# Front of an encoder layer: a fifth gate unit's first products among the last transposes, weight sums behind token sums, tables made 25 products later

## The chip, the cores and the metric

The kernel runs on one core of a Trainium2 chip. The metric is the device time of one execution in microseconds, as the median of several runs. One execution was also taken by the hardware profiler, and every view below is of that one.

## What is computed

One encoder layer on 1024 tokens of 1024 features, in 32-bit floats. Only the first line matters for this change; the rest is cut.

```python
u = rms_norm(h, norm_mix)
proj = u @ w_in                       # 1024 x 3328
z_pool, q, k, v, g_pool, g_attn = split(proj)
y_pool = multiscale_pool(z_pool, w_pool_group, pool_scale) @ w_pool_branch
y_attn = windowed_gqa(q, k, v, sink) @ w_attn_branch
h = h + (sigmoid(g_pool) * y_pool + sigmoid(g_attn) * y_attn) @ w_out
...
```

## The kernel before

**The input projection** is cut into 13 units of 256 output columns: eight gate units ("g", 0) to ("g", 7), z01 and z23 (pooled branch), kv, q01 and q23. Each unit is a 2 x 2 block product (token halves by feature halves) done with seven products instead of eight, in the order `ORDER = ("P1", "P2", "P5", "P6", "P7", "P3", "P4")`. P1 and P2 take the transposed first token half as it is (A11, A12). The other five take sums of the halves: S1, S2, S3, S4 and A22. Some of the weight blocks must be subtracted from each other too; `less` in `block_weights` (L142) does that on GpSimd.

**Each 32-bit operand is split** into a high part (a cast on ScalarE, L84) and a low part (what is left, a subtraction on VectorE, L85, or on GpSimd for the first four weight chunks). One product is 4 blocks of 128 features by 3 matmuls (high by high, high by low, low by high), so 12 matmuls of 512 columns in TensorE (L181). The list `sequence` gives the order of all products; `ahead(n)` loads and splits the weights of the next n of them.

**The front** is the loop over eight rows of 128 tokens, t = 0 to 7. For each row: load x, square and sum it on ScalarE (L417), one over the root on GpSimd (L233), scale by it and by the gain on VectorE (the tile ut, L421), then transpose in TensorE (L379) into one PSUM bank per 512 features, and split that bank. Rows 0 to 3 give A11 and A12. Rows 4 to 7 meet the rows 0 to 3 that were kept (f1, f2 are the halves of the kept row, u1, u2 those of the new one):

```python
        to("S1", combine(s, u1, u2, ALU.add))
        to("A22", u2)
        d = combine(u1, f1, u1, ALU.subtract)
        to("S3", d)
        s2 = combine(f1, s, f1, ALU.subtract)
        to("S2", s2)
        to("S4", combine(f2, f2, s2, ALU.subtract, nc.vector))
```

The first three sums (the token sums s, d and s2) are on GpSimd, the last on VectorE (L392 for all four). Between the transposes stand products that need A11 and A12 alone: P1 and P2 of units 0 to 3. A gate unit's P2 ends in a sigmoid on ScalarE (L301) into the one buffer c11, and a store from there to DRAM. After the loop come P5 of unit 0 and all others; from there on TensorE has operands for everything.

**Small tables** are made after the loop: the distance table for the attention bias (an iota on GpSimd, L449, and four VectorE operations, L450 to L453), the negated sink logits (L459), the pooled branch's weights (L461 to L465) and the counts at its edges (L466 to L474).

**What sets the order.** The framework traces the program, and a scheduler writes one queue per engine when the kernel is built. Each engine runs its queue in that order, and waits at the first instruction whose operands or buffers are not there. `tc.issue_after(ins)` puts what is traced under it behind `ins`, for instructions on the engine of `ins` alone. Tiles of one tag share `bufs` buffers: ut has six, so rows 6 and 7 take buffers that earlier rows have left; the eight PSUM banks are shared by products and transposes.

## Time and profile before

| | |
|---|---|
| time, median of 3 runs | 1187.93 us (1187.76 to 1191.13) |
| time of the profiled execution | 1189.52 us |
| its span, first to last instruction | 1187.7 us |
| TensorE busy | 1155.4 us, 97% |
| VectorE, ScalarE, GpSimd busy | 852.8, 531.2, 484.4 us |

The time of the profiled execution is its span and 1.8 us around it; it lies 1.6 us above the median. Engines are named as in the profile: PE is TensorE, DVE VectorE, ACT ScalarE, POOL GpSimd, SP the engine that issues most loads. L numbers are lines of the kernel before. An operation's row says when it began and how long it took, and in brackets how long the engine had been idle and what ended that.

### The profile page before, as it was taken

Reading aid. Unit: us, or ns where it says so; the run is one execution under the profiler, and the core shown is the slowest. Engines: PE = TensorE matmul, PEld = TensorE weight load, DVE = VectorE, ACT = ScalarE, POOL = GpSimd, SP = SyncE. Lnnn points to the kernel's source line nnn. Section 1 sums busy time; section 2 is a strip of 40 time slices with the busy share of each in tenths; the row PEclk is TensorE's granted clock in tenths of the full one; section 3 lists DMA queues with packets and bytes.
Section 4 is the critical chain, followed back from the end, with each engine's and each line's share of the span. In section 5 each row is a group of like instructions: output and inputs, shape, how many; then the busy total and the mean of one; then the engine's idle time right before and its main releaser. Section 6 shows DMA issues by size and latency. Waiting matters only on the chain.

```text
span 1187.7 us, 15579 instructions
## 1 busy us (share of the span) xinstructions
PE 1155.4 (97%) x5284; PEld 957.7 (81%) x5284; DVE 852.8 (72%) x1297; ACT 531.2 (45%) x1017; POOL 484.4 (41%) x451
## 2 busy tenths in 40 slices
PE   7899999999999999999999999999999999999995
PEld 6788888888888878888778888888888878888884
DVE  6944697765999795549878776777777774665773
ACT  6534345545677544536323333332333344454453
POOL 6833344453545551204444644555544620020230
PEclk9999999999999999999999999999999999999998
DMA  6334235138531665624355543544445357655472
GB/s 213 102 121 137 77 124 180 51 109 303 178 116 45 193 202 190 228 87 152 98 194 191 174 158 128 194 159 160 150 160 179 132 208 268 243 196 193 159 253 84
DMA packets 135347, 192.65 MB, mean 162 GB/s; under 512 B 8866, under 2 KB 87714, under 8 KB 135268
## 3 DMA queue, kind: packets, MB, share of 16 engines
q1 hardware_dynamic: 124276, 157.85, 40.8%
q0 software_dynamic: 7440, 24.39, 5.5%
q10 hardware_dynamic: 3552, 9.44, 2.2%
q8 instruction: 41, 0.67, 0.2%
q14 instruction: 38, 0.31, 0.1%
HBM read 136.85 MB, written 54.79 MB: 161 GB/s over the span
## 4 chain that ended last, share of the span: by engine, by line
PE 83%; DVE 9%; DMA 3%; issue 3%; ACT 1%; POOL 1%; SPq 0%; POOLq 0%; DVEq 0%; ACTq 0%
PE dn L828 17%; PE Z L181 14%; PE X L181 13%; PE Y L181 13%; PE wo L981 7%; PE W L181 7%; DVE wlo L85 2%; PE br L213 2%; PE br L214 2%; PE br L212 2%; DMA sums<-in_w_ffn_down_dram 2%; PE pt L669 1%; PE sc L646 1%; PE pv L682 1%; PE sc L645 1%
## 5 line engine op out<-in xcount | busy, mean ns | idle before, releaser
L84 ACT CAST whi<-raw 128x512 fp32r<-128x512 f32 x378 | 231.2, 619 | 347.0 <-POOL raw L142 79.5
L85 DVE TENSOR_TENSOR wlo<-raw,whi 128x512 fp32r<-128x512 f32 x358 | 323.4, 911 | 63.3 <-ACT whi L84 58.1
L142 POOL TENSOR_TENSOR raw<-raw 128x512 f32<-128x512 f32 x140 | 192.5, 1377 | 229.9 <-DVE wlo L85 191.5
L828 PE MATMUL dn<-wlo,ah 128*128 128x512 f32 x308 | 119.8, 389 | 0.3 <-DVE wlo L85 0.3
L828 PE MATMUL dn<-whi,ah 128*128 128x512 f32 x308 | 117.7, 389 | 1.0 <-ACT ah L84 1.0
L828 PE MATMUL dn<-whi,al 128*128 128x512 f32 x308 | 118.2, 389 | 0.0
L85 DVE TENSOR_TENSOR al<-ab,ah 128x512 fp32r<-128x512 f32 x69 | 48.6, 704 | 67.8 <-ACT ah L84 67.7
L84 ACT CAST ah<-ab 128x512 fp32r<-128x512 f32 x69 | 42.9, 622 | 87.9 <-PE dn L828 87.7
L181 PE MATMUL X<-S_hi,wlo 128*128 128x512 f32 x192 | 75.6, 393 | 0.2 <-DVE wlo L85 0.2
L1053 DVE TENSOR_TENSOR sums<-sums 128x256 f32<-128x256 f32 x88 | 51.0, 580 | 34.0 <-DMA sums<-in_w_ffn_down_dram 30.2
L181 PE MATMUL X<-S_lo,whi 128*128 128x512 f32 x192 | 75.4, 393 | 0.0
L181 PE MATMUL X<-S_hi,whi 128*128 128x512 f32 x192 | 75.3, 392 | 0.0
L181 PE MATMUL Z<-a,whi 128*128 128x512 f32 (+1 forms) x240 | 70.4, 378 | 0.1
L181 PE MATMUL Z<-A_hi,whi 128*128 128x512 f32 x176 | 68.7, 390 | 0.0
L181 PE MATMUL Z<-A_lo,whi 128*128 128x512 f32 x176 | 68.7, 390 | 0.0
L828 PEld LDWEIGHTS dn<-whi,ah 128*128 128x128 f32 x308 | 57.8, 188 | 13.3 <-ACT ah L84 1.4
L181 PE MATMUL Z<-A_hi,wlo 128*128 128x512 f32 x176 | 68.5, 389 | 0.0
L828 PEld LDWEIGHTS dn<-wlo,ah 128*128 128x128 f32 x308 | 57.8, 188 | 12.8 <-DVE wlo L85 0.8
L828 PEld LDWEIGHTS dn<-whi,al 128*128 128x128 f32 x308 | 57.8, 188 | 12.0
L181 PE MATMUL W<-S,whi 128*128 128x512 f32 x176 | 54.6, 391 | 1.8 <-ACT S L84 1.8
L1206 POOL TENSOR_TENSOR o<-o,gain_fin 128x512 f32<-128x512 f32 x8 | 12.4, 1569 | 106.1 <-ACT junk L903 106.1
L659 POOL TENSOR_SCALAR s<-s,den 128x384 f32<-128x384 f32 (+1 forms) x32 | 39.0, 1229 | 38.9 <-DVE den L657 29.3
(265 smaller groups left out, 2802.0 us busy)
## 6 DMA issues: line engine op xcount, KB each, us to landing
ab<-act_dram SPq DMA_DIRECT2D x31, 512.0 KB, 4.0
raw<-in_w_in_dram SPq DMA_DIRECT2D x26, 512.0 KB, 3.8
raw<-in_w_ffn_gate_dram SPq DMA_DIRECT2D x22, 512.0 KB, 4.3
raw<-in_w_ffn_up_dram SPq DMA_DIRECT2D x22, 512.0 KB, 3.9
sums<-in_w_ffn_down_dram SPq DMA_DIRECT2D x44, 256.0 KB, 4.6
wt_dram<-sums SPq DMA_DIRECT2D x22, 512.0 KB, 2.8
act_dram<-sums POOLq DMA_DIRECT2D x44, 256.0 KB, 2.8
raw<-wt_dram SPq DMA_DIRECT2D x20, 512.0 KB, 4.4
```

What stands on the lines that cost most here:

```text
L84: ins = nc.scalar.copy(out=hi, in_=src)
L85: (eng or nc.vector).tensor_tensor(out=lo, in0=src, in1=as32(hi), op=ALU.subtract)
L142: nc.gpsimd.tensor_tensor(out=out, in0=x0, in1=x1, op=ALU.subtract)
L181: nc.tensor.matmul(ps, wt[:, c], at[:, k, cols], start=opening and k == 0 and i == 0, stop=k == 3 and i == 2, skip_group_check=not opening)
L212: nc.tensor.matmul(ps, wh, xh, start=first, stop=False)
L213: nc.tensor.matmul(ps, wh, xl, start=False, stop=False)
L214: nc.tensor.matmul(ps, wl, xh, start=False, stop=last)
L659: (nc.gpsimd if i in POOL_HEADS else nc.vector).tensor_scalar(out=s[:, i, :W], in0=s[:, i, :W], scalar1=den[:, i:i + 1], scalar2=None, op0 ...
L828: nc.tensor.matmul(ps[t], at[:, ts], wt, start=opening and k == 0 and e == 0, stop=k == nk - 1 and e == 2, skip_group_check=not opening)
L981: nc.tensor.matmul(ps[t], at[:, k, ts], wt, start=k == 0 and e == 0, stop=k == KT - 1 and e == 2)
L1053: nc.vector.tensor_tensor(out=out, in0=in0, in1=in1, op=op)
L1206: nc.gpsimd.tensor_tensor(out=o[t][:, :HALF], in0=o[t][:, :HALF], in1=gain3[:, :HALF], op=ALU.mult)
```

## The change

**Products.** Gate unit 4 becomes a fifth early unit: its P1 is traced in row 7 between the transposes for S3 and S2, its P2 right after the loop. Its five other products come after those of units 0 and 1; those of units 2 and 3 move behind z23. The products of row t, for t from 4, are traced ahead of the row's transposes and no longer behind them. The count of products is the same. The tile s1 of the fifth unit gets a pool of its own, and goes before the pooled branch's tiles are made.

**GpSimd.** The weight subtractions of early units are put behind the token sum that was traced last.

**Tables.** Their code moves into `open_pooled`, called before P1 of z01; on VectorE they stand behind the addition of unit 4's P6.

**Squares.** The square's unused result is written to the row's ut tile, not to a tile of its own, and the copies of the gain stand behind both halves of row 0.

```diff
         def less(out, x0, x1):
-            nc.gpsimd.tensor_tensor(out=out, in0=x0, in1=x1, op=ALU.subtract)
+            with ExitStack() as stack:
+                if unit in early_units and "sum" in state:
+                    stack.enter_context(tc.issue_after(state["sum"]))
+                nc.gpsimd.tensor_tensor(out=out, in0=x0, in1=x1, op=ALU.subtract)
             return out
...
         elif prod == "P6":
-            nc.vector.tensor_tensor(out=sb[unit, "s1"], in0=ps, in1=sb[unit, "s1"], **add)
+            state["add"] = nc.vector.tensor_tensor(out=sb[unit, "s1"], in0=ps, in1=sb[unit, "s1"], **add).ins
...
-    early_units = [("g", i) for i in range(4)]
+    early_units = [("g", i) for i in range(5)]
...
     sequence = [(u, p) for i in range(2) for p in ORDER[:2] for u in early_units[2 * i:2 * i + 2]]
+    sequence += [(early_units[4], p) for p in ORDER[:2]]
     sequence += [(u, p) for p in ORDER[2:] for u in early_units[:2]]
-    sequence += [(u, p) for u in early_units[2:] for p in ORDER[2:]]
-    for u in ("z01", "z23", ("g", 4), ("g", 5), "kv", "q01"):
-        sequence += [(u, p) for p in ORDER]
+    for u in (early_units[4], "z01", "z23", early_units[2], early_units[3], ("g", 5), "kv", "q01"):
+        sequence += [(u, p) for p in ORDER[2 if u in early_units else 0:]]
...
     def in_tile(tag, unit):
+        if (tag, unit) == ("s1", early_units[4]):
+            return fifth.tile([P, HALF], F32, name="s1")
...
+    fifth = tc.alloc_tile_pool(name="fifth", bufs=1)
     xin = tc.alloc_tile_pool(name="xin", bufs=1)
...
         def combine(out, in0, in1, op, eng=nc.gpsimd):
-            eng.tensor_tensor(out=out, in0=in0, in1=in1, op=op)
+            ins = eng.tensor_tensor(out=out, in0=in0, in1=in1, op=op).ins
+            if eng is nc.gpsimd:
+                state["sum"] = ins
             return out
...
         to("S3", d)
+        if t == 7:
+            in_product(*sequence[8])
+            ahead(1)
         s2 = combine(f1, s, f1, ALU.subtract)
...
-        junk = xin.tile([P, D], F32, tag="junk", bufs=1, name="junk")
+        ut = xin.tile([P, D], F32, tag="ut", bufs=6, name="ut")
         ssq = small.tile([P, 1], F32, tag="ssq", bufs=2, name="ssq")
...
-            nc.scalar.activation(out=junk, in_=xt, func=AF.Square, accum_out=ssq)
+            nc.scalar.activation(out=ut, in_=xt, func=AF.Square, accum_out=ssq)
         rstd = rstd_of(ssq)
-        ut = xin.tile([P, D], F32, tag="ut", bufs=6, name="ut")
...
         if t == 0:
-            for half in range(2):
-                nc.vector.tensor_copy(out=gain[:, half_of(half)], in_=gains[half])
+            with tc.issue_after(normed):
+                for half in range(2):
+                    nc.vector.tensor_copy(out=gain[:, half_of(half)], in_=gains[half])
+        if t >= 4:
+            in_product(*sequence[t])
+            ahead(1)
         block_columns(t, ut)
...
-        if t >= 4:
-            in_product(*sequence[t])
-            ahead(1)
+    in_product(*sequence[9])
+    ahead(1)
     xin.release()
...
+    def open_pooled():
...
+        both = const.tile([P, D], F32, tag="gain", bufs=1, name="dist")
+        dist, far = pooled["dist"] = both[:, :3 * P], both[:, 3 * P:6 * P]
+        dist_i = far.bitcast(I32)
+        with tc.issue_after(state["add"]):
+            nc.vector.tensor_scalar(out=nsink, in0=sink_b, scalar1=-1.0, scalar2=None, op0=ALU.mult)
+            split(wg_raw, *wg)
+            nc.vector.tensor_copy(out=edge_n, in_=edge_i)
+            nc.vector.reciprocal(out=edge_n, in_=edge_n)
+            nc.gpsimd.iota(dist_i, pattern=[[-1, 3 * P]], base=P, channel_multiplier=1)
+            nc.vector.tensor_copy(out=dist, in_=dist_i)
+            nc.vector.tensor_scalar(out=far, in0=dist, scalar1=-1.0, scalar2=None, op0=ALU.mult)
+            nc.vector.tensor_tensor(out=dist, in0=dist, in1=far, op=ALU.max)
+            nc.vector.tensor_scalar(out=far, in0=dist, scalar1=float(P), scalar2=-NEG, op0=ALU.is_gt, op1=ALU.mult)
...
-        if i < NT:
+        if i < NT + 2:
             continue
+        if (unit, prod) == ("z01", "P1"):
+            fifth.release()
+            open_pooled()
```


**In the order, first: VectorE and ScalarE, rows 5 to 7.** Rows 4, 5, 6 and 7 are the tiles ut_407, ut_479, ut_552 and ut_625 before. On VectorE the S4 sum of row 5 is written in ut_204, the kept row 1:

```order
L421 SCALAR_TENSOR_TENSOR ut_552<-xt_324,rstd_550,gain_mix_89 128x1024
L85 TENSOR_TENSOR A22_lo_118<-tp_418,A22_hi_117 128x4x128
L85 TENSOR_TENSOR S3_lo_114<-tp_426,S3_hi_113 128x4x128
L85 TENSOR_TENSOR S2_lo_112<-tp_434,S2_hi_111 128x4x128
L421 SCALAR_TENSOR_TENSOR ut_625<-xt_449,rstd_623,gain_mix_89 128x1024
L85 TENSOR_TENSOR wlo_397<-raw_394,whi_396 128x512
L392 TENSOR_TENSOR ut_204<-ut_204 128x512
L85 TENSOR_TENSOR S4_lo_116<-tp_442,S4_hi_115 128x4x128
```

With the change rows 4 to 7 are ut_399, ut_470, ut_539 and ut_608, and the kept row 1 is ut_199:

```order
L85 TENSOR_TENSOR wlo_390<-raw_387,whi_389 128x512
L85 TENSOR_TENSOR S1_lo_110<-tp_430,S1_hi_109 128x4x128
L398 TENSOR_TENSOR ut_199<-ut_199 128x512
L85 TENSOR_TENSOR A22_lo_118<-tp_437,A22_hi_117 128x4x128
L85 TENSOR_TENSOR S3_lo_114<-tp_445,S3_hi_113 128x4x128
L234 TENSOR_SCALAR ms_542<-ssq_540 128x1
L85 TENSOR_TENSOR wlo_396<-raw_393,whi_395 128x512
L431 SCALAR_TENSOR_TENSOR ut_539<-xt_323,rstd_544,gain_mix_89 128x1024
```

The S4 sum of row 5 stood behind the scaling of rows 6 and 7 and a weight split; now it stands ahead of the scaling of row 6, and that of row 7 comes nine instructions later still. On ScalarE the squares of rows 6 and 7 stood ahead of the first transposes of row 4:

```order
L84 CAST a1_107<-tp_317 128x4x128
L417 ACTIVATE junk_545,ssq_546<-xt_324 128x1024
L417 ACTIVATE junk_618,ssq_619<-xt_449 128x1024
L84 CAST S1_hi_109<-tp_411 128x4x128
L84 CAST whi_384<-raw_382 128x512
```

With the change row 6's square is behind the high parts of row 4, and row 7's stands here, behind the sigmoids of units 0 and 1 (c11_363 and c11_378 share one buffer):

```order
L306 ACTIVATE c11_363<-Z_223 128x512
L84 CAST whi_424<-raw_422 128x512
L306 ACTIVATE c11_378<-Z_238 128x512
L84 CAST whi_495<-raw_493 128x512
L190 COPY s1_420<-Z_407 128x512
L84 CAST S2_hi_111<-tp_453 128x4x128
L84 CAST S4_hi_115<-tp_461 128x4x128
L428 ACTIVATE ut_608,ssq_609<-xt_468 128x1024
L84 CAST whi_564<-raw_562 128x512
```

So a weight cast, a copy and two high parts now lie between the second sigmoid and the square of row 7.

**Second: GpSimd, at the start and in row 7.** At the start, one over the root of row 2 (rstd_281) stood behind the low parts of two weight chunks:

```order
L233 TENSOR_TENSOR rstd_202<-ms_200,mhalf_87 128x1
L85 TENSOR_TENSOR wlo_172<-raw_169,whi_171 128x512
L85 TENSOR_TENSOR wlo_178<-raw_175,whi_177 128x512
L233 TENSOR_TENSOR rstd_281<-ms_279,mhalf_87 128x1
L85 TENSOR_TENSOR wlo_186<-raw_183,whi_185 128x512
L85 TENSOR_TENSOR wlo_192<-raw_189,whi_191 128x512
```

With the change (rstd_282):

```order
L236 TENSOR_TENSOR rstd_204<-ms_202,mhalf_87 128x1
L85 TENSOR_TENSOR wlo_174<-raw_171,whi_173 128x512
L85 TENSOR_TENSOR wlo_180<-raw_177,whi_179 128x512
L85 TENSOR_TENSOR wlo_188<-raw_185,whi_187 128x512
L236 TENSOR_TENSOR rstd_282<-ms_280,mhalf_87 128x1
L85 TENSOR_TENSOR wlo_194<-raw_191,whi_193 128x512
```

It is now behind three of them. In row 7 the token sums s_627, ut_625 (d) and ut_308 (s2) stood among weight subtractions (raw) before:

```order
L392 TENSOR_TENSOR s_627<-ut_625 128x512
L142 TENSOR_TENSOR raw_536<-raw_538,raw_536 128x4x128
L142 TENSOR_TENSOR raw_609<-raw_609 128x4x128
L392 TENSOR_TENSOR ut_625<-ut_308,ut_625 128x512
L142 TENSOR_TENSOR raw_538<-raw_538,raw_536 128x4x128
L142 TENSOR_TENSOR raw_609<-raw_611,raw_609 128x4x128
L392 TENSOR_TENSOR ut_308<-s_627,ut_308 128x512
```

With the change they are s_640, ut_608 and ut_301:

```order
L236 TENSOR_TENSOR rstd_613<-ms_611,mhalf_87 128x1
L398 TENSOR_TENSOR s_640<-ut_608 128x512
L487 IOTA dist_1057 128x384
L398 TENSOR_TENSOR ut_608<-ut_301,ut_608 128x512
L145 TENSOR_TENSOR raw_679<-raw_679 128x4x128
L398 TENSOR_TENSOR ut_301<-s_640,ut_301 128x512
L145 TENSOR_TENSOR raw_631<-raw_633,raw_631 128x4x128 x2
```

One weight subtraction is left among them where four were, and the iota, which stood in row 6; the other subtractions follow behind s2.

**Third: the end of the front on TensorE.** Before, the transposes of s2 (tp_652) and of the S4 sum (tp_660) of row 7 stand next to each other, behind the last early product:

```order
L379 MATMUL tp_644<-ident_90,ut_625 128x128 x4
L181 MATMUL Z_521<-a1_108,whi_468 128x512
L181 MATMUL Z_521<-a1_107,wlo_469 128x512
...
L181 MATMUL Z_521<-a1_107,wlo_469 128x512
L379 MATMUL tp_652<-ident_90,ut_308 128x128 x4
L379 MATMUL tp_660<-ident_90,ut_308 128x128 x4
L181 MATMUL X_721<-S1_hi_109,whi_541 128x512
```

With the change (tp_657 for d, tp_689 for s2, tp_697 for the S4 sum):

```order
L385 MATMUL tp_657<-ident_90,ut_608 128x128 x4
L184 MATMUL Z_664<-a1_107,whi_495 128x512
L184 MATMUL Z_664<-a1_108,whi_495 128x512
L184 MATMUL Z_664<-a1_107,wlo_496 128x512
...
L184 MATMUL Z_664<-a1_107,wlo_496 128x512
L385 MATMUL tp_689<-ident_90,ut_301 128x128 x4
L385 MATMUL tp_697<-ident_90,ut_301 128x128 x4
L184 MATMUL X_728<-S1_hi_109,whi_636 128x512
L184 MATMUL X_748<-S1_hi_109,whi_684 128x512
```

Twelve matmuls, P1 of unit 4 (Z_664), now stand between the transposes of d and of s2; its P2 follows among the products of P5.

## Rows read from the trace of the kernel before

**Rows 1.** The page: the span, and busy time of each engine.
```profile
span 1187.7 us, 15579 instructions
...
PE 1155.4 (97%) x5284; PEld 957.7 (81%) x5284; DVE 852.8 (72%) x1297; ACT 531.2 (45%) x1017; POOL 484.4 (41%) x451
```

**Rows 2.** TensorE's waits, whole run: waiter, releaser, total us, times, longest.
```profile
PE tp L379 <- DVE ut L392: 5.0, 2, 2.5
```

**Rows 3.** Busy time by stretch: PE, PEld, DVE, ACT, POOL, clock, DMA share, GB/s.
```profile
40.37:44.04 3.67, 3.67 (x12) 2.87 (x10) 3.67 (x5) 0.59 (x1) 3.04 (x3) 0.55 0.60 181
...
57.44:61.13 3.69, 3.69 (x12) 2.87 (x11) 2.52 (x6) 0.74 (x2) 0.98 (x14) 0.55 0.45 144
```

**Rows 4.** Timeline of TensorE: start, us, engine, line, what, count, idle before.
```profile
15.30 1.97 PE L379 MATMUL tp<-ident,ut 128*128 128x128 f32 x8 [1.07 <-DVE ut L421]
...
39.95 0.66 PE L379 MATMUL tp<-ident,ut 128*128 128x128 f32 x4 [2.52 <-DVE ut L392]
40.37 0.89 PE L181 MATMUL Z<-a,whi 128*128 128x512 f32 x2
...
44.78 0.60 PE L379 MATMUL tp<-ident,s 128*128 128x128 f32 x4
...
57.05 0.63 PE L379 MATMUL tp<-ident,ut 128*128 128x128 f32 x4 [2.51 <-DVE ut L392]
57.44 0.48 PE L181 MATMUL X<-S_hi,whi 128*128 128x512 f32 x1
...
64.60 0.39 PE L181 MATMUL W<-S_hi,whi 128*128 128x512 f32 x1
...
70.04 0.39 PE L181 MATMUL Y<-S_hi,whi 128*128 128x512 f32 x1
```

**Rows 5.** Timeline of VectorE, 12 to 57 us.
```profile
12.96 2.29 DVE L421 SCALAR_TENSOR_TENSOR ut<-xt,rstd,gain_mix 128x1024 f32<-128x1024 f32 x1
...
34.54 1.99 DVE L421 SCALAR_TENSOR_TENSOR ut<-xt,rstd,gain_mix 128x1024 f32<-128x1024 f32 x1
36.46 1.76 DVE L85 TENSOR_TENSOR wlo<-raw,whi 128x512 fp32r<-128x512 f32 x1
38.15 1.75 DVE L392 TENSOR_TENSOR ut<-ut 128x512 f32<-128x512 f32 x1
...
47.88 1.65 DVE L452 TENSOR_TENSOR dist<-dist 128x384 f32<-128x384 f32 x1
...
56.23 0.68 DVE L392 TENSOR_TENSOR ut<-ut 128x512 f32<-128x512 f32 x1
```

**Rows 6.** Timeline of GpSimd, 12 to 53 us.
```profile
12.38 0.54 POOL L233 TENSOR_TENSOR rstd<-ms,mhalf 128x1 f32<-128x1 f32 x1
12.89 3.49 POOL L85 TENSOR_TENSOR wlo<-raw,whi 128x512 fp32r<-128x512 f32 x2
...
37.62 0.45 POOL L449 IOTA dist<- 128x384 int32 x1
...
47.36 3.31 POOL L142 TENSOR_TENSOR raw<-raw 128x512 f32<-128x512 f32 x2
50.64 1.40 POOL L392 TENSOR_TENSOR ut<-s,ut 128x512 f32<-128x512 f32 x1
```

**Rows 7.** Timeline of ScalarE, 31 to 37 us.
```profile
31.65 1.28 ACT L301 ACT_TABLE_LOAD   x1
32.95 0.60 ACT L301 ACTIVATE c<-Z 128x512 f32<-128x512 f32 x1
...
36.30 0.60 ACT L301 ACTIVATE c<-Z 128x512 f32<-128x512 f32 x1 [1.76 <-DMA g_dram<-c]
```

**Rows 8.** Tile xt: min, median, max ns of its readers; time to landing.
```profile
L417 ACT ACTIVATE junk<-xt x7: 1057/1062/1067, 7.0 to 25.4; 128x1024 f32<-128x1024 f32 x7
...
L421 DVE SCALAR_TENSOR_TENSOR ut<-xt,rstd,gain_mix x5: 1283/1592/2290, 9.7 to 23.6; 128x1024 f32<-128x1024 f32 x5
...
DMA to landing us min/median/max: 3.1/4.3/6.4
```

More of the change, by code (lines that the diff above doesn't have):

```diff
@@ L412, in encoder_kernel @@
             for i in range(2):
-                nc.scalar.activation(out=junk[:, half_of(i)], in_=xt[:, half_of(i)], func=AF.Square,
+                nc.scalar.activation(out=ut[:, half_of(i)], in_=xt[:, half_of(i)], func=AF.Square,
                                      accum_out=sq2[:, i:i + 1])
@@ L440, in encoder_kernel @@
                 ahead(3)
-        if t >= 4:
-            in_product(*sequence[t])
-            ahead(1)
+    in_product(*sequence[9])
+    ahead(1)
     xin.release()
     later.append(tc.alloc_tile_pool(name="st2", bufs=1, side="right"))
-    both = const.tile([P, D], F32, tag="gain", bufs=1, name="dist")
-    dist, far = both[:, :3 * P], both[:, 3 * P:6 * P]
-    dist_i = far.bitcast(I32)
-    nc.gpsimd.iota(dist_i, pattern=[[-1, 3 * P]], base=P, channel_multiplier=1)
-    nc.vector.tensor_copy(out=dist, in_=dist_i)
@@ L473, in encoder_kernel @@
-    nc.vector.tensor_copy(out=edge_n, in_=edge_i)
-    nc.vector.reciprocal(out=edge_n, in_=edge_n)
+    pooled = {}
+    def open_pooled():
+        zp = pooled["zp"] = tc.alloc_tile_pool(name="zp", bufs=1)
+        wg_raw = zp.tile([P, HALF], F32, tag="p", bufs=3, name="wg_raw").rearrange("p (g d) -> p g d", g=4)
+        wg = pooled["wg"] = [zp.tile([P, 4, P], F32R, name="wg_" + part) for part in ("hi", "lo")]
+        edge_n = pooled["edge_n"] = zp.tile([P, 4, 2, PAD], F32, name="edge_n")
+        edge_i = zp.tile([P, 4, 2, PAD], I32, name="edge_i")
+        nc.sync.dma_start(out=sink_b, in_=sink[0:1, :].partition_broadcast(P))
+        nc.sync.dma_start(out=psc, in_=pool_scale.rearrange("o (g p) -> p (o g)", p=P))
+        nc.sync.dma_start(out=wg_raw, in_=w_pool_group[0].rearrange("g c d -> c g d"))
+        nc.gpsimd.memset(edge_i, 1)
+        for g, w in enumerate(POOL_WINDOWS):
+            nc.gpsimd.iota(edge_i[:, g, 0, :w // 2], pattern=[[1, w // 2]], base=w // 2, channel_multiplier=0)
+            if w > 2:
+                nc.gpsimd.iota(edge_i[:, g, 1, :w // 2 - 1], pattern=[[-1, w // 2 - 1]], base=w - 1,
+                               channel_multiplier=0)
+        both = const.tile([P, D], F32, tag="gain", bufs=1, name="dist")
[11 more added lines that the diff above has]
+            nc.vector.tensor_scalar(out=far, in0=dist, scalar1=float(P), scalar2=-NEG, op0=ALU.is_gt, op1=ALU.mult)
@@ L512, in windows @@
             ps = bank("gm")
-            mm3(ps, wg_hi[:, g], wg_lo[:, g], d_hi[:, sl], d_lo[:, sl], True, True)
-            hi, lo = [zp.tile([P, HALF], F32, tag="p", bufs=3, name="p").bitcast(F32R) for _ in range(2)]
+            mm3(ps, *[part[:, g] for part in pooled["wg"]], d_hi[:, sl], d_lo[:, sl], True, True)
+            hi, lo = [pooled["zp"].tile([P, HALF], F32, tag="p", bufs=3, name="p").bitcast(F32R) for _ in range(2)]
             split(ps, hi, lo, scale=psc[:, g:g + 1])
@@ L543, in encoder_kernel @@
                     pass
-            zp.release()
+            pooled["zp"].release()
             att = tc.alloc_tile_pool(name="att", bufs=1)
@@ L624, in encoder_kernel @@
     sm = tc.alloc_tile_pool(name="sm", bufs=1)
+    dist, far = pooled["dist"]
     def bias_of(g):
```

34 lines of the change are left out of this document (7 added, 27 removed).

## The prediction

> **What bounds the kernel.** I read the page first: TensorE is busy 97% of the span [rows 1], so only its idle time, and time at a lower clock, can be won. Then its waits: the longest group of the whole run is transposes that wait for the VectorE line that makes the S4 sums, two waits with 5.0 us in all [rows 2]. Then the timeline around them: the waits are 2.52 us before 39.95 and 2.51 us before 57.05 [rows 4]. Then the windows behind them: in both the granted clock is 0.55 of full speed [rows 3], close to the lower of TensorE's two levels, 1.2 of 2.4 GHz; what the engine did just before was to stand idle. In the timeline [rows 4] the twelve matmuls from 40.37 to 44.78 took 4.41 us, and the 24 from 57.44 to 64.60 took 7.16; at full speed 24 took 5.44 (64.60 to 70.04), so twelve take 2.72. The low clock cost 4.41 - 2.72 = 1.69 and 7.16 - 5.44 = 1.72 us. The two places together hold 5.03 + 3.41 = **8.44 us**.
>
> Why the waits are there is in the queues. Ahead of the first, VectorE does the scaling of row 7 and a weight split before the S4 sum of row 5, all three slow, 1.99, 1.76 and 1.75 us [rows 5], while the same sum took 0.68 at 56.23. Ahead of the second, GpSimd spends 3.31 us on two weight subtractions before s2 of row 7, which ends at 52.04 [rows 6]; VectorE reaches its S4 sum at 56.23 [rows 5], and nothing but transposes is left for TensorE to do.
>
> **The change part by part.**
>
> *The first wait goes (2.52 + 1.69 us).* The S4 sum of row 5 moves ahead of the scaling of rows 6 and 7, and a whole product of twelve matmuls (P1 and P2 are ready early) now lies before row 5's transposes. I take the whole of it; the lower bound is that the new queue ahead of row 5's last transposes gives the wait back.
>
> *The second wait goes (2.51 + 1.72 us).* The fifth unit's P1, 2.72 us of work at full speed, stands between the transposes of d and s2. It is not extra work: it leaves a later stage in which TensorE has no wait of this size [rows 2], so the end comes earlier by what it covers here.
>
> *The start gets later (1.05 us lost).* One over the root of row 2 started at 12.38 and took 0.54 [rows 6]. It now has one more low part ahead, 3.49 / 2 = 1.75 us beside VectorE [rows 6], or about 1.3 without it, so the scaling of row 2 starts 1.3 to 1.75 us later than 12.96. It has then one low part beside it and no longer two: between the free 1.28 [rows 8] and the 2.29 it took [rows 5]. It ends between 12.96 + 1.3 + 1.28 = 15.5 and 12.96 + 1.75 + 2.29 = 17.0; before, 15.25. TensorE waits for it at 15.30 [rows 4]. That is 0.3 to 1.75 us later; I take the middle. From there to the first wait TensorE works without a pause, so the delay is carried on.
>
> *Tables and gain copies: nothing.* VectorE loses four table operations, the longest 1.65 us [rows 5], at a place where it is never idle (3.67 of 3.67 us in the first window of [rows 3]); that helps the row 7 chain below and is not counted by itself. In the later place, between unit 4 and z01, TensorE has no wait of the size of [rows 2], so there is cover; without it they would cost at most four times 1.76 [rows 5], spread over five products. The iota (0.45 [rows 6]) stays in front of d of row 7; it is counted below.
>
> *Squares.* The square's result now goes into ut, whose buffers come free only when earlier rows are transposed. So rows 6 and 7 are squared late. This is the new chain, and it must be on time. Its steps, for row 7:
> - The first sigmoid comes later than 32.95 by the 1.05 above and two matmuls of 512 columns that now go first (2 x 0.23): 34.45, end 35.05. The second waits until the first's store has landed. Before, that took 36.30 - 33.55 = 2.75 us [rows 7], so it starts at 37.8.
> - Five ScalarE operations of 0.6 [rows 7], then the square, 1.06 [rows 8]: 41.9. One over the root 0.54 [rows 6]: 42.4. Up to two VectorE operations of 0.7 ahead of the scaling: 43.8. Scaling 1.28 to 2.29 [rows 8]: 45.1 to 46.1.
> - On GpSimd s, iota, d: 1.40 + 0.45 + 1.40 [rows 6]: d is ready at 48.4 to 49.4. One weight subtraction (3.31 / 2 = 1.66) and s2 (1.40): 51.4 to 52.5. The S4 sum 0.68 to 1.75 [rows 5]: 52.1 to 54.2.
>
> When are they needed? If TensorE never waits, W starts at 64.60 - 8.44 + 1.05 + 5.44 = 62.65, as 24 more matmuls lie before it. Back from there: 36 matmuls (24 of X, twelve of unit 4's P2) at 5.44 / 24 = 0.227 give 54.5 for the first X; eight transposes (four took 57.44 - 57.05 = 0.39) give 53.7 for those of s2 and 54.1 for those of the S4 sum; twelve matmuls and four transposes give 50.6 for those of d. All are met: by 1.2 to 2.2 us for d and s2, by 2.0 down to nothing for the S4 sum.
>
> The square of row 7 now follows a sigmoid, which needed a table load of 1.28 us [rows 7]; the order of the changed kernel has no further load between them, so I count none. The Trainium skill (ScalarE: Activation LUTs, Table sets: the hidden batching unit) speaks against such mixing: functions should be batched by table set, and every change of set loads again. By its figure of about 2.66 us a switch (the page What ACT_TABLE_LOAD costs in the same notes), two switches would put an estimated 5.3 us into the chain; no run here shows a square behind a sigmoid.
>
> **The sum.** 8.44 - 1.05 = 7.4 us. The profiled execution took 1189.52 us, its span and 1.8 around it; it would come to 1182.1. It lies 1.6 us above the median of the runs, 1187.93, and against that the forecast is **1180.5 us**. About 0.3%, 3.6 us, is what a measurement of this kernel tells from no change: faster is below 1184.4, slower above 1191.5.
>
> **The rivals.**
>
> - *A smaller wait stays in the front.* TensorE waits at row 7's S4 sum, at row 5's transposes (whose PSUM bank is held until the second sigmoid has read it), or for row 5's x, whose load stands behind two more weight loads; landing takes 3.1 to 6.4 us, median 4.3 [rows 8]. For it: two bounds above meet with nothing to spare. Price: a wait of 1 to 2.5 us and one stretch at low clock, 1.7: gain 7.4 - 2.7 = 4.7 down to 7.4 - 4.2 = 3.2, so 1183.2 to 1184.7.
> - *The gain is given back.* Both, the start at its late bound (1.75) and two such waits with their clock: 8.44 - 1.75 - 2 x (1.7 + 1.7) is about 0, 1188. For it: VectorE has no idle time there, and the change adds two weight splits of up to 1.76 us [rows 5]. Against: it removes the tables and most of GpSimd's work beside it.
> - *The row 7 chain becomes the bound, and it is slower.* Place: ScalarE's queue, where the square of row 7 is behind the second sigmoid and that behind a store. Each us that d is later than 50.6 is a us of wait, and the first brings the low clock (1.7) with it. The gain of 7.4 is gone when the chain is 1.2 + 5.7 = 6.9 us later than worked out, and it is slower by 3.6 at 10.5: 1191.5 and more. For it: this chain did not exist before, row 7 was scaled at 34.54 [rows 5]. Against: the store would have to take 2.75 + 10.5 = 13 us.
> - *Table loads.* If squares and sigmoids needed different tables, two loads of 1.28 [rows 7] would lie in that chain: 2.6 us against 1.2 spare, a wait of 1.4 and the clock, 1.7; gain 4.3, 1183.6. This is the rule of the Trainium skill named above.
> - *The change does not do what it says.* The order shows that products, sums and squares did move, so only the iota stays where it was; its 0.45 is counted.
>
> **How the numbers follow.** Forecast, gain 5.6 to 8.4: 0.70. A smaller wait 0.13, table loads 0.03: both faster, or at the edge of no change. Given back 0.10. Slower 0.04. Of the 0.16 of the smaller wait and the table loads I put 0.10 on faster and 0.06 on no change, where all of "given back" goes. So faster 0.80, no change 0.16, slower 0.04. The range goes from 1178.5 (the start costs 0.3 and the runs come out a little lower than the median) to 1186.0, which takes in the smaller wait and the table loads, and leaves out what is given back and what is slower.
>
> **What would show it.** In the changed profile: no wait of transposes for VectorE's S4 sums above 1 us; granted clock near full from 25 to 65 us; the transposes of row 2 at about 16.4; the second sigmoid 2.8 us behind the first; the scaling of row 7 at 44 and its s2 at 50 to 51; W from 62 to 63; all beyond shifted by 7 us. It is wrong if TensorE waits in row 5 or row 7 and the clock falls there, if the start costs more than 2 us, or if a later stage gives the time back.

## The result, and the profile after

| | before | after |
|---|---|---|
| time, median (5 runs each, on one chip) | 1189.99 us (1187.76 to 1191.13) | 1183.99 us (1182.55 to 1184.10) |
| profiled execution: time, span | 1189.52, 1187.7 us | 1183.99, 1182.2 us |

The ratio of the times is 0.9947, with an interval of 0.9936 to 0.9957: the change makes the kernel 6.3 us faster (5.1 to 7.6). By the bound of 0.3% this is faster. The forecast of 1180.5 us is 3.5 us too low, but inside its range. Of the 3.5 us, 2.1 lie in the kernel before, whose median came out at 1189.99 us beside the changed kernel and not at the 1187.93 it was worked from.

The page of the changed kernel, span and busy times (to be set beside [rows 1]):

```profile
span 1182.2 us, 15578 instructions
...
PE 1152.8 (98%) x5284; PEld 954.9 (81%) x5284; DVE 852.8 (72%) x1297; ACT 530.3 (45%) x1017; POOL 484.8 (41%) x451
```

The span is 5.5 us shorter. VectorE's busy time is the same to a tenth: no work was saved, it was moved. TensorE in three windows (busy time, granted clock, share of the DMA engines, GB/s), against the 0.55 of [rows 3]:

```profile
20.00:40.00 20.00, 20.00 (x147) 1.00 0.43 124
40.00:60.00 20.00, 19.00 (x109) 1.00 0.37 116
60.00:80.00 20.00, 20.00 (x90) 1.00 0.37 109
```

The clock stays at full speed in these 60 us, and TensorE is idle for 1.00 of them. Its timeline, at the places of [rows 4] (start, duration, what it did, in brackets the idle time before it and what ended that):

```profile
4.30 3.75 PE L373 MATMUL gain<-gain_row,ones 1*128 1x512 f32 x4 [4.30 <-DMA gain_row<-in_norm_mix_dram]
...
12.80 1.97 PE L385 MATMUL tp<-ident,ut 128*128 128x128 f32 x8 [2.40 <-DVE ms L234]
...
16.76 1.97 PE L385 MATMUL tp<-ident,ut 128*128 128x128 f32 x8 [1.17 <-DVE ms L234]
...
22.14 1.03 PE L385 MATMUL tp<-ident,ut 128*128 128x128 f32 x8
...
54.21 1.03 PE L385 MATMUL tp<-ident,ut 128*128 128x128 f32 x8
55.00 0.71 PE L184 MATMUL X<-S_hi,whi 128*128 128x512 f32 x2
56.63 0.50 PE L184 MATMUL X<-S_lo,whi 128*128 128x512 f32 x1 [0.93 <-DVE S_lo L85]
...
64.48 0.39 PE L184 MATMUL W<-S_hi,whi 128*128 128x512 f32 x1
```

Both waits for the S4 sums are gone; the last transposes follow at 54.21 without a pause. One wait is new: the first product X, two matmuls after its start, waits 0.93 us for a low part. Why, VectorE's queue shows:

```profile
45.17 1.27 DVE L431 SCALAR_TENSOR_TENSOR ut<-xt,rstd,gain_mix 128x1024 f32<-128x1024 f32 x1
...
52.51 1.77 DVE L398 TENSOR_TENSOR ut<-ut 128x512 f32<-128x512 f32 x1
54.20 0.68 DVE L85 TENSOR_TENSOR S_lo<-tp,S_hi 128x512 fp32r<-128x512 f32 x1
54.81 1.17 DVE L85 TENSOR_TENSOR wlo<-raw,whi 128x512 fp32r<-128x512 f32 x1
55.90 0.68 DVE L85 TENSOR_TENSOR S_lo<-tp,S_hi 128x512 fp32r<-128x512 f32 x1
```

The first token sum of row 7 has its low part at 55.90, behind the S4 sum (1.77 us), another low part and a weight's low part (1.17). From 45 to 60 us VectorE has no pause. GpSimd in the same stretch:

```profile
46.59 1.28 POOL L398 TENSOR_TENSOR s<-ut 128x512 f32<-128x512 f32 x1 [2.13 <-DVE ut L431]
47.82 0.45 POOL L487 IOTA dist<- 128x384 int32 x1
48.24 1.29 POOL L398 TENSOR_TENSOR ut<-ut 128x512 f32<-128x512 f32 x1
49.49 1.73 POOL L145 TENSOR_TENSOR raw<-raw 128x512 f32<-128x512 f32 x1
51.17 1.30 POOL L398 TENSOR_TENSOR ut<-s,ut 128x512 f32<-128x512 f32 x1
```

The sum s of row 7 waits 2.13 us for the scaling; iota, d, one weight subtraction and s2 follow as the forecast had them. And ScalarE:

```profile
33.03 1.28 ACT L306 ACT_TABLE_LOAD   x1
34.33 0.60 ACT L306 ACTIVATE c<-Z 128x512 f32<-128x512 f32 x1
...
37.15 0.60 ACT L306 ACTIVATE c<-Z 128x512 f32<-128x512 f32 x1 [1.71 <-DMA g_dram<-c]
...
39.58 1.10 ACT L428 ACTIVATE ut<-xt 128x1024 f32<-128x1024 f32 x1
```

The square of row 7 runs at 39.58, after two sigmoids, and no table is loaded between them.

### The profile page after: what moved, and what is told of

It is laid out like the page before. It is cut to its first block, busy times and chain, and to the rows that moved or that the text cites. A ratio compares the mean times of both kernels' runs of the same rounds, so it can differ in the third digit from the quotient of the medians.

```text
span 1182.2 us, 15578 instructions
## 1 busy us (share of the span) xinstructions
PE 1152.8 (98%) x5284; PEld 954.9 (81%) x5284; DVE 852.8 (72%) x1297; ACT 530.3 (45%) x1017; POOL 484.8 (41%) x451
## 4 chain that ended last, share of the span: by engine, by line
PE 89%; DVE 5%; DMA 2%; issue 2%; ACT 1%; POOL 0%; SPq 0%; POOLq 0%; DVEq 0%; ACTq 0%
PE dn L850 17%; PE Z L184 15%; PE Y L184 15%; PE X L184 14%; PE wo L1003 7%; PE W L184 7%; PE br L216 2%; PE br L217 2%; PE br L215 2%; PE pt L691 1%; DVE wlo L85 1%; PE tp L385 1%; DMA sums<-in_w_ffn_down_dram 1%; PE pv L704 1%; PE sc L668 1%
## 5 line engine op out<-in xcount | busy, mean ns | idle before, releaser
L145 POOL TENSOR_TENSOR raw<-raw 128x512 f32<-128x512 f32 x140 | 195.9, 1402 | 228.6 <-DVE wlo L85 183.1
```

Source lines behind the costliest of these rows:

```text
L145: nc.gpsimd.tensor_tensor(out=out, in0=x0, in1=x1, op=ALU.subtract)
```

## The experiments

All runs stand beside runs of the kernel before on the same chip, five or more executions of each kernel. The quantity to look at is when W of unit 0 begins, counted from the first matmul: by then every kernel but the ninth has done the same work (the ninth, like the kernel before, 24 matmuls or 5.44 us less). It is read from one execution of each kernel, and two things at the start change from run to run: the landing of x's second row, whose square began between 6.76 and 8.76 us, and how soon TensorE gets fast (its matmuls of 256 columns took 0.41 us at first and 0.28 later; the first short one came 2.8 to 5.6 us behind the start of row 2's transposes). So the transposes of row 2 are given too, and the time from row 3's transposes to W: between rows 2 and 3 every kernel does the same work, and row 3 came behind the first short matmul in every run. Line numbers in rows are those of the kernel that ran.

| kernel | ratio to before (interval) | first matmul to row 2 | first matmul to W | row 3 to W | waits from 25 us to W |
|---|---|---|---|---|---|
| before | 1 | 11.34 | 60.64 | 43.50 | 2.52, 2.51 |
| changed | 0.9947 (0.9936 to 0.9957) | 12.46 | 60.18 | 42.34 | 0.93 |
| 1 free copies | 0.9943 (0.9930 to 0.9955) | 11.29 | 59.32 | 42.89 | 0.30, 0.93 |
| 2 S1 low first | 0.9941 (0.9927 to 0.9954) | 13.06 | 59.39 | 41.25 | none |
| 3 both | 0.9937 (0.9924 to 0.9949) | 11.73 | 58.64 | 41.78 | 0.30 |
| 4 fifth unit's P1 late | 0.9962 (0.9949 to 0.9974) | 13.08 | 61.18 | 42.49 | 1.59 |
| 5 tables early | 0.9977 (0.9967 to 0.9987) | 12.72 | 63.14 | 45.38 | 1.42, 0.63, 0.32 |
| 6 sums free | 0.9968 (0.9956 to 0.9980) | 12.35 | 61.93 | 44.39 | 0.97, 0.56, 0.97 |
| 7 products behind | 0.9935 (0.9922 to 0.9947) | 13.67 | 59.85 | 40.16 | none |
| 8 squares early | 0.9954 (0.9942 to 0.9967) | 14.36 | 62.79 | 43.06 | 0.33, 1.70 |
| 9 late squares alone | 1.0023 (1.0014 to 1.0032) | 11.14 | 62.25 | 46.26 | 1.72, 0.45, 0.33, 2.65, 1.47 |
| 10 early and behind | 0.9966 (0.9954 to 0.9979) | 12.42 | 62.05 | 44.18 | 0.97, 0.76 |
| 11 behind, free copies | 0.9924 (0.9912 to 0.9937) | 11.27 | 58.04 | 41.63 | 0.57 |
| 12 as 11, S1 low first | 0.9924 (0.9910 to 0.9937) | 11.18 | 57.90 | 41.33 | 0.57 |

### 1. Free copies of the gain

```diff
-            with tc.issue_after(normed):
-                for half in range(2):
-                    nc.vector.tensor_copy(out=gain[:, half_of(half)], in_=gains[half])
+            for half in range(2):
+                nc.vector.tensor_copy(out=gain[:, half_of(half)], in_=gains[half])
```

> The changed kernel with one part undone: the two copies of the gain are again free to run between the two halves of row 0. With that the queues of the start stand as in the kernel before: one over the root of row 2 is behind two low parts on GpSimd and no longer three, and row 1's scaling is ahead of the first split. In the changed kernel the transposes of row 2 began 12.46 us after the first matmul (16.76 - 4.30), in the kernel before 11.34 (15.30 - 3.96); those of row 3 began 17.84 after it (before 17.14). My theory: the start was lost in these two queues. Row 2's transposes then begin 11.2 to 11.5 us after the first matmul, row 3's 17.1, and as TensorE works without a pause from there, W of unit 0 begins 0.7 us earlier after the first matmul than the 60.18 of the changed kernel: 59.5. Ratio to the kernel before 0.9941 instead of 0.9947. Rival: what was lost at the start is hidden by the wait for the first sum's low part (0.93 us at 56.63), which only grows by what the start gives back: W stays at 60.2 and the time at 0.9947.

TensorE's timeline of this kernel: first matmul, row 2's transposes, the wait in X, and W:

```profile
4.04 3.75 PE L373 MATMUL gain<-gain_row,ones 1*128 1x512 f32 x4 [4.04 <-DMA gain_row<-in_norm_mix_dram]
...
15.33 1.97 PE L385 MATMUL tp<-ident,ut 128*128 128x128 f32 x8 [1.03 <-DVE ut L431]
...
55.51 0.50 PE L184 MATMUL X<-S_lo,whi 128*128 128x512 f32 x1 [0.93 <-DVE S_lo L85]
...
63.36 0.39 PE L184 MATMUL W<-S_hi,whi 128*128 128x512 f32 x1
```

The start is back to that of the kernel before: 11.29 us to row 2. In the four kernels with free copies (1, 3, 11 and 12) row 2 began 11.18 to 11.73 us after the first matmul, in the eight with tied copies 12.35 to 14.36. W comes 0.86 us earlier: row 3 was 1.41 us earlier, and 0.55 of that went again behind row 3, 0.30 of it in a new wait. The wait in X is 0.93 as it was. So the start was lost in the two queues, and the wait in X does not swallow what is won there. The two copies were enough: with them free the scheduler put one over the root of row 2 ahead of the third low part again. The time itself, 0.4 permille less, is within the interval.

### 2 and 3. Row 7's first low part ahead of a weight's

```diff
         to("S1", combine(s, u1, u2, ALU.add))
+        s1_low = state["vlow"]
...
             in_product(*sequence[8])
+            state["low"] = s1_low
             ahead(1)
```

In `split`, VectorE's next low part of a weight is then put behind `s1_low`; `vlow` is the low part traced last. The third kernel has this and the free copies.

> The changed kernel with two neighbours on VectorE exchanged: the low part of row 7's first token sum goes ahead of the low part of the next unit's weight (1.17 us in the changed kernel), nothing else moves on any engine. My theory: the 0.93 us that TensorE waited in the first product X (56.63) is the queue on VectorE alone. The low part then ends at 55.5 instead of 56.6, the wait shrinks to 0.1 or nothing, W of unit 0 begins 59.3 us after the first matmul (60.18 in the changed kernel), ratio to the kernel before 0.9940. Rival: VectorE is short of time as a whole there (it has no pause from 45 to 60 us), so the wait goes to the next consumer, the weight's low part in unit 1's X or a later low part, and W stays at 60.2.

> Both edits of the two kernels before this one. If both are separate losses and add up: W of unit 0 begins 60.18 - 0.7 - 0.85 = 58.6 us after the first matmul, the time is 1.5 us under that of the changed kernel, ratio to the kernel before 0.9934. If VectorE as a whole is the limit at the end of the front, the two do not add: W at 59.3 to 59.5.

In the second kernel the wait in X is gone and none takes its place; W comes 0.79 us earlier although row 2 was 0.60 later; from row 3 on it is 1.09. In the third, W is at 58.64, as expected for two separate losses that add (58.6). Queue order was the cause of this wait, not VectorE's amount of work.

### 4. The fifth unit's P1 behind the loop

```diff
-        if t == 7:
-            in_product(*sequence[8])
-            ahead(1)
...
-    in_product(*sequence[9])
-    ahead(1)
+    for i in range(8, 10):
+        in_product(*sequence[i])
+        ahead(1)
```

> The changed kernel with the fifth unit's P1 traced behind the loop and no longer between the transposes of d and s2 of row 7. All 24 matmuls of P1 and P2 are still in the front, but behind the last transposes; the weight subtraction ahead of s2 on GpSimd goes too. My theory (this product covers the second wait): the transposes of s2 and the S4 sum come up 2.7 us earlier, at 51.4, s2 is ready at 50.8 and the S4 sum at 52 to 52.5, so 0.6 to 1.1 us of wait come back, without a drop of the clock if it is short; W of unit 0 begins 60.8 to 61.3 us after the first matmul, with the clock's loss 62.5 to 63. Rival: the second wait went because GpSimd's token sums no longer stand behind weight sums, and the product's place is worth nothing: no wait for the S4 sum, W at 60.2, ratio 0.9947.

The one wait in TensorE's timeline of this kernel:

```profile
53.64 0.66 PE L385 MATMUL tp<-ident,ut 128*128 128x128 f32 x4 [1.59 <-DVE S_lo L85]
```

and VectorE's queue ahead of it:

```profile
51.25 1.74 DVE L398 TENSOR_TENSOR ut<-ut 128x512 f32<-128x512 f32 x1
52.91 1.88 DVE L85 TENSOR_TENSOR S_lo<-tp,S_hi 128x512 fp32r<-128x512 f32 x3
```

A wait of 1.59 us comes back and the clock stays at 1.00. VectorE ends the S4 sum at 52.99, but the transposes begin at 53.64 only, when the first of the low parts behind it has read its PSUM bank: the bank was late, not the sum. W is 1.00 us later, but 0.85 of that lies ahead of row 3's transposes, where this edit moves nothing; behind them it is 0.15, with a wait of 1.59 in place of 0.93. The ratios differ by 1.8 us (0.9962 against 0.9947), and their intervals overlap. So the place of P1 is worth little of the 4.2 us that the forecast gave it.

### 5. Tables early

The iota and the four VectorE operations of the distance table stand behind the loop again, without `issue_after`.

> The changed kernel with one part undone: the distance table is made behind the loop again, so its four VectorE operations (0.35, 0.34, 1.65 and 0.84 us in the kernel before) stand among the splits of rows 6 and 7, ahead of row 7's S4 sum; nothing else moves. The prediction counted this part at nothing by itself. My theory now: VectorE has no pause from 45 to 60 us in the changed kernel, so each us of it there goes into the end of the front: 2.9 to 3.2 us of wait at the S4 transposes or in X, in pieces, W of unit 0 at 63.1 to 63.4 us after the first matmul (60.18 in the changed kernel), 64.8 to 65.1 if a wait of over 2 us brings the low clock; ratio to the kernel before 0.997 to 0.998. Rival (as predicted): VectorE has slack there and the tables' place is worth under 0.5 us: W at 60.2 to 60.7, ratio 0.9947.

TensorE's waits in this kernel's timeline:

```profile
51.72 0.63 PE L385 MATMUL tp<-ident,ut 128*128 128x128 f32 x4 [1.42 <-DVE S_lo L85]
52.97 0.74 PE L184 MATMUL Z<-a,whi 128*128 128x512 f32 x2 [0.63 <-DVE A_lo L85]
...
59.26 0.50 PE L184 MATMUL X<-S_lo,whi 128*128 128x512 f32 x1 [0.32 <-DVE S_lo L85]
```

Its windows there (columns as above):

```profile
53.00:56.00 3.00, 3.00 (x9) 0.67 0.16 61
56.00:60.00 4.00, 3.68 (x17) 0.82 0.00 0
```

The four table operations on VectorE:

```profile
49.55 1.42 DVE L466 CAST dist<-dist 128x384 f32<-128x384 int32 x1
...
51.49 0.83 DVE L467 TENSOR_SCALAR dist<-dist 128x384 f32<-128x384 f32 x1
...
52.84 1.03 DVE L468 TENSOR_TENSOR dist<-dist 128x384 f32<-128x384 f32 x1
...
54.39 0.83 DVE L469 TENSOR_SCALAR dist<-dist 128x384 f32<-128x384 f32 x1
```

They take 4.1 us where they took 3.2 in the kernel before; TensorE waits three times (2.37 us together, against 0.93), and behind the first two waits the granted clock is 0.67 and 0.82 in the next windows. W is 2.96 us later (3.04 from row 3), of which 1.44 is wait and the rest is about what a stretch of low clock cost in the kernel before, 1.7. No other single part that was undone cost as much, and the forecast had put nothing on it.

### 6. Sums free

```diff
-                if unit in early_units and "sum" in state:
-                    stack.enter_context(tc.issue_after(state["sum"]))
```

> The changed kernel without the order between GpSimd's token sums and the weight sums of early units. One weight subtraction then stands ahead of s2 of row 6, two more ahead of s of row 7, 1.3 to 1.7 us each. My theory: d of row 7, which ended at 49.5 and was needed about 50.6, is 2 to 3 us later, and s2 and the S4 sum behind it; the transposes of row 7 wait 1 to 2.5 us in all, W of unit 0 at 61.2 to 62.7 us after the first matmul, ratio 0.9955 to 0.997; with a drop of the clock 1.7 more. Rival: the fifth unit's product covers it, the order is worth nothing, W at 60.2.

Row 7's transposes wait 0.97 for s, 0.56 for d and 0.97 for the S4 sum. W is 1.75 us later (2.05 from row 3), in the middle of what was expected. The order of GpSimd's sums is needed.

### 7. Products behind the transposes

```diff
-        if t >= 4:
-            in_product(*sequence[t])
-            ahead(1)
         block_columns(t, ut)
...
+        if t >= 4:
+            in_product(*sequence[t])
+            ahead(1)
```

In this kernel the fourth unit's P2 and the fifth unit's P1 use each other's weights, since weights are handed out in the order in which products are traced; amount and shape of the work are unchanged, but what this kernel computes is not the layer.

> The changed kernel with the products of rows 4 to 7 traced behind their transposes again, all else as changed. The S4 sum of row 5 is then no longer ahead of the scaling of rows 6 and 7 on VectorE. My theory: the first wait returns, 2 to 2.5 us near 40 us, and with it the low clock (1.7 us): W of unit 0 at 63.9 to 64.4 us after the first matmul, ratio 0.998. Rival: the first wait went with the other edits (late squares, sums ahead on GpSimd), W at 60.2 to 60.7.

My theory failed: TensorE does not wait once between row 3 and W, at row 5 or anywhere else, and the kernel is if anything faster than the changed one: from row 3 to W it takes 2.18 us less, of which a late start leaves 0.33 at W. The place that the prediction held to be the cure of the first wait is not needed for it.

### 8. Squares early

```diff
-        ut = xin.tile([P, D], F32, tag="ut", bufs=6, name="ut")
+        junk = xin.tile([P, D], F32, tag="junk", bufs=1, name="junk")
...
-            nc.scalar.activation(out=ut, in_=xt, func=AF.Square, accum_out=ssq)
+            nc.scalar.activation(out=junk, in_=xt, func=AF.Square, accum_out=ssq)
         rstd = rstd_of(ssq)
+        ut = xin.tile([P, D], F32, tag="ut", bufs=6, name="ut")
```

> The changed kernel with one part undone: the squares are written to a tile of their own again, so rows 6 and 7 are squared as soon as x is there. My prediction saw the late squares as the new chain, with 1.2 us to spare for d and s2. If the chain still decides something (the 0.93 us in X), early squares take it away: W of unit 0 at 59.3 us after the first matmul, ratio 0.994. If the work of VectorE alone decides, nothing changes: W at 60.2. Below nothing: the scaling of row 6 and 7 now comes ahead of S4 sums again on VectorE and a wait of up to 1 us may come in row 4 or 5.

No first wait here either. W is 2.61 us later, but 1.90 of that lies ahead of row 2's transposes, where x's second row landed late (its square began at 8.76 and not 7.22). Behind them it is 0.7, with a wait of 1.70 in place of 0.93. So the late squares were no burden; undoing them gives nothing.

### 9 and 10. One suspect alone, and both undone

The ninth is the kernel before with the squares written into ut, and no other edit. The tenth is the changed kernel with both of the last two undone (with the fourth unit's P2 between d and s2, and the fifth unit's P1 behind the last transposes, each with its own weights):

```diff
         if t == 7:
-            in_product(*sequence[8])
+            in_product(*sequence[7])
...
+        if t >= 4:
+            in_product(*sequence[t + (t == 7)])
+            ahead(1)
```

> The kernel before with one part of the change alone: the squares are written into ut, so rows 6 and 7 are squared and scaled late; products, sums and tables stand as before. My theory after the last runs (no single part undone brought the first wait back): two parts each remove it, the late squares (the scaling of rows 6 and 7 then comes behind row 5's S4 sum on VectorE) and the products ahead of the transposes. Late squares alone then take away the wait near 40 us and its clock (4.2 us), but row 7's chain, behind GpSimd's weight sums and with the tables on VectorE, comes later, so the second wait stays or grows, 2.5 to 5 us: ratio to the kernel before 0.996 to 1.000. Rival (my prediction: the products' place removes the first wait): a wait of over 1 us before 42 us stays.

> The changed kernel with both suspects undone: squares in a tile of their own (early), and the products of rows 4 to 7 behind their transposes (the product between d and s2 of row 7 is then the fourth unit's P2, that of the fifth unit's P1 comes behind the last transposes). The order of GpSimd's sums, the fifth unit and the late tables stay. If either part was enough by itself, the first wait is back here: 1 to 2.5 us at row 5's S4 transposes between 36 and 42 us, W of unit 0 at 60.9 to 63 us after the first matmul, more with a drop of the clock. Rival: the order on GpSimd removed it; then no wait over 0.5 us between 30 and 45 us, W at 59 to 60.

The ninth kernel's longest waits, in TensorE's timeline:

```profile
43.80 1.31 PE L379 MATMUL tp<-ident,ut 128*128 128x128 f32 x8 [1.72 <-DVE S_lo L85]
...
56.32 1.12 PE L379 MATMUL tp<-ident,ut 128*128 128x128 f32 x4 [2.65 <-POOL ut L392]
58.90 1.09 PE L379 MATMUL tp<-ident,ut 128*128 128x128 f32 x4 [1.47 <-DVE ut L392]
```

Late squares alone leave no wait ahead of 42 us, as the theory said. But then TensorE waits 1.72 us one row later, for a low part of row 6 that stands behind three weight splits (36.91, 4.02 us) and the scaling of row 7 (40.85, 2.30 us) on VectorE. It waits 2.65 for GpSimd, which still has weight sums ahead of s2, and 1.47 for row 7's S4 sum, and the kernel is 0.23% slower than before. The tenth kernel's waits:

```profile
39.11 0.63 PE L385 MATMUL tp<-ident,ut 128*128 128x128 f32 x4 [0.97 <-DVE S_lo L85]
40.50 0.63 PE L385 MATMUL tp<-ident,ut 128*128 128x128 f32 x4 [0.76 <-DVE ut L398]
```

VectorE ahead of them:

```profile
36.05 2.32 DVE L432 SCALAR_TENSOR_TENSOR ut<-xt,rstd,gain_mix 128x1024 f32<-128x1024 f32 x1
38.29 1.27 DVE L85 TENSOR_TENSOR S_lo<-tp,S_hi 128x512 fp32r<-128x512 f32 x2
39.49 0.87 DVE L398 TENSOR_TENSOR ut<-ut 128x512 f32<-128x512 f32 x1
```

and TensorE's window behind them:

```profile
41.00:44.00 3.00, 3.00 (x11) 0.57 0.27 38
```

The first wait is back in two pieces, 0.97 and 0.76 us, ahead of row 5's transposes of s2 and of the S4 sum: the scaling of row 7 (36.05, 2.32 us) stands ahead of a low part and of the S4 sum on VectorE, and the clock is at 0.57 behind it. So **in the changed kernel either part is enough to remove the first wait** (kernels 7, 8 and 10), and undoing only one cannot show it. In the kernel before, the late squares alone moved VectorE's delay to the next row.

### 11 and 12. A faster arrangement

The edits of kernels 1 and 10, but with squares late; the twelfth has that of kernel 2 too.

> The changed kernel with two parts undone: free copies of the gain (the start as before) and the products of rows 4 to 7 behind their transposes (the fourth unit's P2 stands between d and s2 of row 7). Late squares, the order of sums and the late tables stay. Against the run with free copies alone (W 59.32 us after the first matmul, with waits of 0.30 and 0.93) it tells what the place of the products is worth. If products ahead only cost (transposes come later, so the splits crowd at the end of the front on VectorE), both waits go: W at 57.9 to 58.3, ratio 0.993. If they are needed, a wait comes back in row 5 and W is at 59.3 or later.

> The kernel before this one with the low part of row 7's first token sum ahead of the weight's low part on VectorE, as in the second run. If the run before this has no wait in X, this one is the same, W at 57.9 to 58.3 us after the first matmul; if it has one, this one is that much faster. Ratio to the kernel before 0.992 to 0.9935, 1 to 3 us under the changed kernel.

The eleventh kernel's first matmul, its only wait, and W, in TensorE's timeline:

```profile
3.86 3.75 PE L373 MATMUL gain<-gain_row,ones 1*128 1x512 f32 x4 [3.86 <-DMA gain_row<-in_norm_mix_dram]
...
44.61 0.63 PE L385 MATMUL tp<-ident,ut 128*128 128x128 f32 x4 [0.57 <-DVE ut L398]
...
61.90 0.39 PE L184 MATMUL W<-S_hi,whi 128*128 128x512 f32 x1
```

Against kernel 1, which differs from kernel 11 only in the products' place, W comes 1.28 us earlier (58.04 against 59.32). The reason is visible in the order of TensorE: a whole product now stands between the last transposes and X, and it covers the splits that X waited for. One wait of 0.57 us is left, and the edit of kernel 2 adds nothing any more. Medians were 1180.98 and 1180.49 us beside 1189.22 for the kernel before: a ratio of 0.9924 (0.9910 to 0.9937), against the changed kernel's 0.9947 (0.9936 to 0.9957). So this arrangement is faster than both kernels of the study, than the changed one by about 2.7 us (their intervals just touch), and in the traces W comes 2.14 and 2.28 us earlier.

## Why the prediction was right, and where it was not

**The outcome held, and the mechanism in the main.** It forecast that both waits and both stretches of low clock go, and they went; W comes 5.56 us earlier for the same work and the span is 5.5 us shorter, so no later stage gave it back. Which edit removed which wait, the forecast had wrong in part, as the paragraphs below show. Its sum did not depend on that, since it priced the two waits and all edits were in: with the tables left in place it would have given the same 1180.5 us, though kernel 5 shows that this costs some 3 us. That much of the hit is luck. The chain of row 7, its new risk, came nearly as worked out: first sigmoid 34.33 (forecast 34.45), second 37.15 (37.8), s2 ready at 52.47 (51.4 to 52.5), S4 sum ready at 54.28 (52.1 to 54.2). The scaling was late, at 45.17 and not 43.8, though the square was early: one over the root of row 7 stood on GpSimd behind row 6's s2 (40.96, 1.28 us) and a weight subtraction (42.21, 1.28 us) and ran from 43.46 for 0.99 us. GpSimd's shorter sums (1.28 us, 1.40 counted) made up for some of it, so that s2 came at the late end of its range.

**The gain of 7.4 us was 5.6 in the profile** (64.60 + 5.44 - 64.48). W begins at 64.48 and not at 62.65. Half of the difference, 0.93 us, is the term that the sum left out: X's wait for the low part of row 7's first sum. The working ended at the S4 sum and did not follow what is queued behind that sum on VectorE, which X needs first. The rival "a smaller wait" named the S4 sum, row 5 and the load of x, not this, and priced it with the clock, which did not fall; so it cost 0.93 and not 2.7 or more. The other 0.9 us is in pieces under 0.3, at single transposes and at the first matmuls behind them; no run shows a cause for them.

**The start: the size was right, the path only in part.** TensorE's rows of the kernel before, to be set beside those of the changed one:

```profile
11.34 1.97 PE L379 MATMUL tp<-ident,ut 128*128 128x128 f32 x8 [1.17 <-DVE ut L421]
...
21.10 1.03 PE L379 MATMUL tp<-ident,ut 128*128 128x128 f32 x8
```

Row 3's transposes began 1.04 us later (22.14 against 21.10), forecast 1.05. But 0.34 of it is the first matmul, whose operand landed later in this run, and 0.70 the change. And the loss does not begin at GpSimd's third low part: row 1's transposes were late already, by 1.12 us counted from the first matmul (12.80 - 4.30 = 8.50, before 11.34 - 3.96 = 7.38), since on VectorE both copies (9.15, 1.28 us) and a low part stood ahead of row 1's scaling, which began at 10.95 and not at 9.69. So the step "Tables and gain copies: nothing" is wrong for the copies: kernel 1 takes the loss away with them alone. That 1.04 met the forecast of 1.05 is luck too: in the eight kernels with tied copies row 3 began 0.4 to 2.6 us later than in the kernel before, counted from the first matmul.

**The same step is wrong for the tables.** The forecast said that their absence helps row 7's chain and counted nothing. Kernel 5 puts them back and loses 2.96 us in the profile and 3.6 by the ratios (0.9977 against 0.9947). They are part of why the second wait is gone; the forecast gave the whole of it to the fifth unit's P1, whose place is worth 0.15 from row 3 to W (kernel 4). The order of GpSimd's sums is worth 2.05 there (kernel 6). The rows of the kernel before held a sign of it: s2 of row 7 was ready at 52.04 [rows 6], but VectorE came to the S4 sum only at 56.23 [rows 5], so its own queue was the last to be waited for.

**The first wait went, but not for the reason given.** The forecast named the S4 sum's place ahead of the scalings and the product ahead of row 5's transposes in one breath, as the work of the products' new order, and the late squares as a risk only. Kernels 7 to 10 show two causes, each of which is enough: the late squares, which put the scalings behind the S4 sum, and the products' place. With the squares late, the products' place costs 1.28 us (kernels 1 and 11; 2.18 from row 3 between the changed kernel and kernel 7).

**Table loads.** The rule of the Trainium skill (ScalarE: Activation LUTs, Table sets: the hidden batching unit) speaks of a load at each change of set; here a square at 39.58 follows a sigmoid at 37.15 with no load between them, so here the two need no change of set. The rival is gone.

## What to carry to other kernels

When several edits are made at one place, cost the place and not the edits: what was credited to one of them (the product between the transposes) came from three, and an undo of a single edit shows nothing where another one covers the same wait. On an engine without a pause, work that nobody waits for has a price too: moving 3.2 us of it away was worth 1.44 us of wait and a stretch of low clock here, and letting the waited-for one of two neighbours go first was worth 1.09, where the other took 1.17. After the last operand on the list, follow the queue on: the next wait was for the operand that stood right behind it.

## What the runs showed that was not expected

- **A wait is not always paid with the clock.** Behind a single wait of 0.93, 1.59 or 1.70 us (changed kernel, kernels 4 and 8) the granted clock stayed at 1.00. Behind 1.42 and 0.63 us with four transposes between them it was 0.67 in the next window (kernel 5), behind 0.97 and 0.76 with four between them 0.57 (kernel 10), and behind 2.52 in the kernel before 0.55 [rows 3]; but behind 0.97 and 0.56 with eight between them it stayed at 1.00 (kernel 6), and behind 1.72 and 0.45 with eight between them it was 0.59 in the window from 45 to 48 us (kernel 9). So two short waits close together can cost what a long one does, and a price of "wait and clock" for every wait, as the rivals had it, is too high for short ones. What decides between these cases, the runs do not show.
- **VectorE's durations depend on GpSimd.** The same table cast took 0.35 us in the kernel before, where GpSimd was idle until 43.35, and 1.42 in kernel 5, where GpSimd was at work on a weight subtraction (rows below, of the kernel before and of kernel 5). The S4 sum, with both inputs in SBUF, took 0.67 to 1.78 us, while low parts of transposes, with one input in PSUM, took 0.67 to 0.69 in every place. The Trainium skill (SBUF — State Buffer, SBUF: two separate sides) says that the two engines share a port pair as a lock, held for a whole instruction, and that VectorE needs it for two SBUF inputs and in its two-port modes; the rows of the sums and of the low parts agree, and whether the cast ran in such a mode no run shows. So work on VectorE has to be priced by what stands beside it, up to four times its shortest row.

```profile
43.19 0.35 DVE L450 CAST dist<-dist 128x384 f32<-128x384 int32 x1
43.35 2.81 POOL L142 TENSOR_TENSOR raw<-raw 128x512 f32<-128x512 f32 x2 [0.63 <-DVE wlo L85]
```

```profile
49.05 1.71 POOL L145 TENSOR_TENSOR raw<-raw 128x512 f32<-128x512 f32 x1
```

- **The start has a spread of its own.** The square of x's second row began at 6.76 to 8.76 us in these runs, and row 0's second half stands behind that row's mean on VectorE (in the changed kernel 8.41, then 8.49), so a late landing of row 1 delays row 0. Exchanging the two was not tried. Small differences of W between two kernels are therefore better read from row 3 on.
